# Value groups of the past behind score blocks, and two of the last eight output tiles on GpSimd

## The chip, the cores and the metric

The kernel runs on one core of one Trainium2 chip, in one launch. The metric is the device time of a whole execution in microseconds (us). Before the change three runs took 1004.15, 1002.61 and 1003.99 us, with a median of 1003.99 us. The profile comes from a further execution of 1003.43 us; its span, from the first to the last recorded instruction, is 1001.8 us, so 1.63 us lie around the span. The mean granted clock of TensorE was 0.998 of full speed.

TensorE (PE) multiplies; a matmul `out<-moving,weights` takes its weights as an array tile, written 128\*128 for the whole array, 64\*128 or 128\*32 for a part of it. VectorE (DVE), ScalarE (ACT) and GpSimd (POOL) work elementwise, SyncE (SP) issues DMAs, and ACT and POOL issue some too.

## The reference

The program computes one inference step of one decoder layer for 512 prompt tokens and 8 samples that share the weights:

```
m  = silu(c) @ ada_w + ada_b                  # shifts, scales, gates
h  = rms_norm(x) * (1 + scale1) + shift1
xr, gr, q, k, v, fl, ga, gb = split(h @ w_in)
ya = (rg_lru(conv(xr)) * gelu(gr)) @ w_proj_a                 # recurrence
yb = forgetting_attention(q, k, v, log_sigmoid(fl)) @ w_proj_b
x  = x + gate1 * ((sigmoid(ga) * ya + sigmoid(gb) * yb) @ w_o)
x  = x + gate2 * swiglu(rms_norm(x) * (1 + scale2) + shift2)
y  = rms_norm(x)
```

The prompt attends to itself, causally. Each of the 8 samples attends to 1024 past rows, which lie in 8 pages of 128 rows each, picked out of `cache_k` and `cache_v` by a page table, and to its own row:

```
s = q . k_all * scale + (decay of the forget gates)
p = softmax(s);   o = p @ v_all
```

The change touches `p @ v_all` for the past of the samples, and the last line, `y = rms_norm(x)`.

## The kernel before, in words

Prompt and samples stand side by side as 520 columns; the 1024 features are 8 tiles of 128 rows. A product of the layer (`product`, line 326) makes one tile of 128 output rows in two halves of 260 columns each. Its numbers are split into a rounded high part and a low rest, so each product is the sum of three: high by high, low by high and high by low. A half has 24 matmuls (`part_product`, L311): 8 steps of depth with three matmuls each.

The past of the samples runs beside these products. Its value pages come in pairs (one page for each of two samples, 512 KB each). A pair is used by one **value group**: `sample_values` (L946) issues 4 matmuls with 32 weight columns each, in array tiles 128\*32, for 512 moving columns (the profile counts 8). 32 groups are to be done, 8 for each of four pairs of samples; after a pair of samples `fold_values` folds the sum (one matmul, recorded as two, tile `pvs`).

What sets the order of the groups: the program is written out in order, and each engine runs its instructions in that order. Every product begins with `begin` (L289); for product n up to 41 it calls `tick(KEYS[n], n in VALUES)`. `tick` (L874) first moves the softmax of the past one step on (its small matmuls write tiles `lgt`, `lgm`, `lgs`), then issues one value group if one is due and its probabilities are there, and then up to KEYS[n] key pages, which DVE multiplies and sums (L857, L858). Right behind a value group the loads of the next pair are issued (`value_pages`, `page_load`): by POOL's queue up to n = 41, by SP's after that. Key pages, value pages and some weights share 7 buffers (`pgp`, tag `pg`), so a load waits until the buffer's last user is done.

From n = 42 on, in a loop over the 8 tiles of the attention, `at(i, part)` takes the place of `begin`'s call; the table VALUES_AT[i][part] says whether a group stands there. Round i of the loop runs on PE in this order:

1. first half of `k` of the next tile; four transposes `vt`; **part 0**; second half of `k`
2. eight transposes `ptt` of the probabilities (`turn(i, 0)`); **part 1**
3. first half of `v`; twelve more `ptt`; score block `sc` 0 and 1 of the next tile; **part 2**; second half of `v`
4. the weighted values `po` (`values`, L1412); score blocks `sc` 2 and 3 of the next tile; **part 3**

Scores and the recurrence's gate products (`gate`, L1130) use array tiles of 64\*128, the products and the transposes the whole 128\*128. After a score block DVE adds the decay and takes the minimum (L1362), ACT takes the exponential (L1363), DVE the reciprocal of the sums (L1365), and ACT, for one head of two POOL, scales the probabilities `p` (L1369), which the transposes `ptt` read.

The end of the kernel is `last_product` (L1671): the last product `fo`, its residual and the final norm, first for 280 columns and then for the 240 others. `norm(1)` gets the sums of squares by PE, their root by ACT (L1710), the reciprocal by DVE, and spreads the factor over 128 rows by PE into the PSUM tile `r3p` (L1715). Then DVE makes the eight tiles of `y` (L1726), two at a time, and SP issues a store for every two (L1727).

Of the kernel before, what the change touches and what calls it, by code (L numbers as in the profile page):

```python
# [12 lines left out]
ALU = mybir.AluOpType  # L13
# [54 lines left out]
def kernel(ctx, tc, xT, par1, par, gates, b_f, cst, cse, own, cache_k, cache_v, cache_lf, pt,  # L68
# [3 lines left out]
    pe, act, dve, pool, sp = nc.tensor, nc.scalar, nc.vector, nc.gpsimd, nc.sync  # L72
# [9 lines left out]
    def slot(name, cols=NT, dt=F32, parts=128):  # L82
        return heap.tile([parts, cols], dt, name=name, tag="slot")

    def bank(name, parts=128, cols=512):
        return psp.tile([parts, cols], F32, name=name, tag="bank")

    def small(name, parts, cols, bufs=4):
        return sm.tile([parts, cols], F32, name=name, tag="s_" + name, bufs=bufs)
# [6 lines left out]
    x = []  # L96
# [97 lines left out]
    def flush():  # L194
        while stores:
            sp.dma_start(*stores.pop(0))
# [2 lines left out]

    KEYS = dict(zip(range(42), (2, 2, 0, 0, 1, 2, 2, 2, 1, 1, 1, 1, 2, 2, 2, 1, 0, 1, 0, 1, 2, 2, 2, 2, 1, 1, 1, 1, 2, 2, 1, 2,  # L200
                                1, 1, 1, 2, 1, 1, 1, 1, 2, 0)))
    VALUES = (19, 21, 23, 25, 27, 29, 31, 35, 37, 39)
    LAST_POOL = 41

    def load_chunks(upto):
        while state["dma"] < len(chunks) and state["dma"] <= upto:
            c = state["dma"]
            if c in joined:
                raw = pgp.tile([128, GROUP, 256], F32, name="wraw", tag="pg")
            else:  # L210
                raw = wp.tile([128, KT, 256], F32, name="wraw", tag="wraw", bufs=2)
            o = 0
            for src, r0, nk, c0, n in chunks[c]:
                sp.dma_start(raw[:, :nk, o:o + n],
                             src[r0:r0 + nk * 128, c0:c0 + n].rearrange("(k p) c -> p k c", p=128))
                o += n
            raws[c] = raw
            state["dma"] += 1
# [59 lines left out]
    def reach(n, last, time):  # L278
        while n < last:
            time -= 1.34 if isinstance(units[n + 1][1], str) else 0.67 * units[n + 1][2]  # L280
            if time < 0:
                break
            n += 1
        return n
# [4 lines left out]
    def begin(last=None):  # L289
        n = state["n"]  # L290
        state["n"] += 1
        last = len(units) - 1 if last is None else last
        if n == 1:
            split_upto(reach(n, last, state["lead"]))
        if n < 42:
            tick(KEYS[n], n in VALUES)
        load_chunks(units[reach(n, last, state["load"])][0])
        split_upto(reach(n, last, state["lead"]))
        flush()
        return n  # L300
# [4 lines left out]
    def part_product(n, t0, t1, a, out, mid=None):  # L305
        hi, lo = splits[n]
        nk = units[n][2]
        for k in range(nk):
            ah, al = a(k) if callable(a) else (v[:, t0:t1] for v in a[k])
            for m, (wt, at) in enumerate(((hi, ah), (lo, ah), (hi, al))):  # L310
                state["mm"] = pe.matmul(out[:, :t1 - t0], lhsT=wt[k], rhs=at, start=k == 0 and m == 0,  # L311
                                        stop=k == nk - 1 and m == 2)
            if mid is not None and k == nk // 2 - 1:
                mid()
# [280 lines left out]
    for f in range(KT):  # L595
        t = slot("sq1")
# [50 lines left out]
    for n in range(6):  # L647
        t0, t1 = HALVES[n % 2]
# [19 lines left out]
    for n in range(6):  # L668
        t0, t1 = HALVES[n % 2]
# [204 lines left out]
    def tick(keys, values):  # L874
        state["age"] = 1 if state["n"] < 5 else 2
        key_sums()
        with in_place():
            for c in list(chains):
                c[0] += 1
                if c[0] >= 2:  # L880
                    c[0] = 0
                    if next(c[1], True):
                        chains.remove(c)
            state["due"] += values
            state["due"] -= some_values(min(1, state["due"]))
        value_pages()
        key_pages(keys)
# [141 lines left out]
    for i in range(KT):  # L1029
        if i % 4 == 0:  # L1030
            qtp.append(bank(f"qt{i}", NS))
        if i < 6:
            t = qpart[i]
# [15 lines left out]
        else:  # L1049
            t = slot("q")  # L1050
# [435 lines left out]
    scores(0, (2, 3))  # L1486
    g = None
    state.update(load=14, lead=8)
    VALUES_AT = [(1, 1, 0, 1)] * 4 + [(1, 1, 0, 0)] + [(1, 1, 0, 1)] * 2 + [(1, 1, 0, 0)]
    KEYS_AT = [(0, 0, 2, 0)] * 3 + [(0, 0, 0, 0)] * 5  # L1490

    def at(i, part):
        tick(KEYS_AT[i][part], VALUES_AT[i][part])
        flush()
# [176 lines left out]
    def last_product(ac):  # L1671
        ss3, r3 = slot("ss3"), slot("r3")
        squares = []
        u = state["n"]

        def done(i, j, t0, t1, b):
            gate, n = mod[:, 5, i], min(t1, NP) - t0
            if j == 0:
                t = small("rs", 128, NS)
                dve.tensor_tensor(t, b[:, n:t1 - t0], gate[:, 1:9], ALU.mult)  # L1680
            dve.scalar_tensor_tensor(x[i][:, t0:t0 + n], b[:, :n], gate[:, 0:1], x[i][:, t0:t0 + n],
                                     ALU.mult, ALU.add)
            if j == 0:
                dve.tensor_tensor(x[i][:, NP:], x[i][:, NP:], t, ALU.add)
            if i == 0:
                act.activation(ss3[:, t0:t1], x[i][:, t0:t1], AF.Square)
            else:
                q_ = heap.tile([128, t1 - t0], F32, name="sq3", tag="slot")
                act.activation(q_, x[i][:, t0:t1], AF.Square)
                if j == 0 or i < 6:  # L1690
                    (pool if j == 0 and i < 5 else dve).tensor_tensor(ss3[:, t0:t1], ss3[:, t0:t1], q_, ALU.add)
                else:
                    squares.append(q_)
            act.activation(x[i][:, t0:t1], x[i][:, t0:t1], AF.Copy, scale=prm[:, i, P_NF:P_NF + 1])

        def norm(j, t0, t1):
            n = t1 - t0
            parts = [ss3[:, t0:t1], *squares]
            r = bank("r3p")[:, :n] if j else r3[:, t0:t1]
            if j:  # L1700
                h_ = n // 2
                ps = [bank(f"r3_{b}", h_, 1) for b in range(2)]
                for k, q_ in enumerate(parts):
                    for b in range(2):
                        pe.matmul(ps[b], lhsT=q_[:, h_ * b:h_ * b + h_], rhs=ones[:, :1], start=k == 0,
                                  stop=k == len(parts) - 1)
                rt = small("rt", h_, 2, 1)
                dg = slot("dg", n, parts=h_)
                for b in range(2):
                    act.activation(rt[:, b:b + 1], ps[b], AF.Sqrt, bias=eps[:h_], scale=1.0 / D)  # L1710
                dve.reciprocal(rt, rt)
                for b in range(2):
                    bs = slice(h_ * b, h_ * b + h_)
                    dve.tensor_scalar(dg[:, bs], ident[:h_, :h_], rt[:, b:b + 1], None, ALU.mult)
                    pe.matmul(r[:, bs], lhsT=ones[:h_, :], rhs=dg[:, bs], start=True, stop=True)  # L1715
            else:
                ps = bank(f"r3_{j}")[:, :n]
                for k, q_ in enumerate(parts):
                    pe.matmul(ps, lhsT=ones, rhs=q_, start=k == 0, stop=k == len(parts) - 1)
                act.activation(r3[:, t0:t1], ps, AF.Sqrt, bias=eps, scale=1.0 / D)  # L1720
                dve.reciprocal(r, r3[:, t0:t1])
            eng = dve if j else pool
            for f0, f1 in ((0, 2), (2, 4), (4, 6), (6, 8)) if j else ((0, 2), (2, 5), (5, 8)):
                y = pgp.tile([128, 3, n], F32, name="y", tag="pg")
                for f in range(f0, f1):
                    eng.tensor_tensor(y[:, f - f0], x[f][:, t0:t1], r, ALU.mult)  # L1726
                sp.dma_start(yT[128 * f0:128 * f1, t0:t1].rearrange("(f p) t -> p f t", p=128), y[:, :f1 - f0])  # L1727

        for j, (t0, t1) in enumerate(LAST_PARTS):
            for i in range(KT):  # L1730
                if j == 0:
                    begin(u + KT - 1)
                b = bank(f"fo{i}_{j}")
                part_product(u + i, t0, t1, ac, b)
                done(i, j, t0, t1, b)
                if j and i == 0:
                    norm(0, *LAST_PARTS[0])
        norm(1, *LAST_PARTS[1])

    def pair_out():  # L1740
# [180 lines left out]
```

## Time and profile before

| what | us |
|---|---|
| runs (three) | 1004.15, 1002.61, 1003.99 |
| profiled execution | 1003.43 |
| its span | 1001.8 |
| PE busy | 984.8 (98% of the span) |
| DVE busy | 778.0 (78%) |
| ACT busy | 553.4 (55%) |
| POOL busy | 344.0 (34%) |

A row of the timeline gives the start of a run of equal instructions, its length, the engine, the line, the operation and its operands, how many there are (x4), and in brackets how long the engine stood idle before it and for whom. Matmuls are pipelined: the length of one is not what it costs. What one costs PE is the distance from its start to the start of the next. A group of instructions (by line or by tile) has the durations of one instruction in ns, least, median and most.

### The profile page before, as it was taken

Reading aid. Unit: us, or ns where it says so; the run is one execution under the profiler, and the core shown is the slowest. Engines: PE = TensorE matmul, PEld = TensorE weight load, DVE = VectorE, ACT = ScalarE, POOL = GpSimd, SP = SyncE. Lnnn points to the kernel's source line nnn. Section 1 sums busy time; section 2 is a strip of 40 time slices with the busy share of each in tenths; the row PEclk is TensorE's granted clock in tenths of the full one; section 3 lists DMA queues with packets and bytes.
Section 4 is the critical chain, followed back from the end, with each engine's and each line's share of the span. In section 5 each row is a group of like instructions: output and inputs, shape, how many; then the busy total and the mean of one; then the engine's idle time right before and its main releaser. Section 6 shows DMA issues by size and latency. Waiting matters only on the chain.

```text
span 1001.8 us, 21578 instructions
## 1 busy us (share of the span) xinstructions
PE 984.8 (98%) x8156; PEld 912.1 (91%) x8156; DVE 778.0 (78%) x1386; ACT 553.4 (55%) x1139; POOL 344.0 (34%) x436
## 2 busy tenths in 40 slices
PE   6999999999999999999999999999999999999996
PEld 5889999999898988888888879999999999999996
DVE  5598999979999878785564545868888888889864
ACT  5434769776951576767772224544444444445553
POOL 0254131323253266554310002394343342434212
PEclk9999999999999999999999999999999999999999
DMA  9998766879879999896667994242424234233212
GB/s 322 330 277 293 228 199 189 278 250 301 266 245 355 329 285 306 284 293 228 215 240 266 338 345 134 59 126 64 126 65 127 82 109 114 56 106 106 64 64 86
DMA packets 164507, 204.04 MB, mean 204 GB/s; under 512 B 9635, under 2 KB 128051, under 8 KB 164339
## 3 DMA queue, kind: packets, MB, share of 16 engines
q1 hardware_dynamic: 148162, 151.14, 48.2%
q0 software_dynamic: 12560, 45.10, 13.3%
q10 hardware_dynamic: 3680, 6.42, 1.7%
q8 instruction: 64, 1.05, 0.4%
q14 instruction: 41, 0.33, 0.1%
HBM read 189.54 MB, written 13.09 MB: 202 GB/s over the span
## 4 chain that ended last, share of the span: by engine, by line
PE 92%; ACT 4%; DVE 2%; DMA 1%; issue 1%; SPq 0%; DVEq 0%; ACTq 0%
PE fo L311 13%; PE wo L311 5%; PE gb L311 5%; PE pa L311 5%; PE xr L311 5%; PE pb L311 4%; PE v L311 4%; PE k L311 4%; PE ga L311 4%; PE gr L311 4%; PE pv L946 3%; PE po L1412 2%; PE sc L1349 2%; PE ada L378 2%; PE ptt L1378 2%; PE fi L311 1%
## 5 line engine op out<-in xcount | busy, mean ns | idle before, releaser
L250 ACT CAST whi<-wraw 128x1024 fp32r<-128x1024 f32 (+1 forms) x79 | 82.0, 1040 | 87.1 <-PE pb L311 34.4
L252 DVE TENSOR_TENSOR wlo<-wraw,whi 128x1024 fp32r<-128x1024 f32 (+1 forms) x79 | 97.4, 1233 | 20.3 <-ACT whi L250 16.9
L274 ACT CAST wb<-ws 128x512 fp32r<-128x512 f32 x72 | 44.7, 621 | 88.7 <-PE fo L311 61.8
L311 PE MATMUL fo<-ach,wb 128*128 128x260 f32 x512 | 93.4, 282 | 0.0
L275 DVE TENSOR_TENSOR wb<-wraw,wb 128x512 fp32r<-128x512 f32 x86 | 78.4, 912 | 5.5 <-ACT wb L274 4.9
L311 PEld LDWEIGHTS fo<-ach,wb 128*128 128x128 f32 x512 | 78.8, 188 | 0.0
L265 POOL TENSOR_TENSOR ws<-wraw 128x512 f32<-128x512 f32 x18 | 23.6, 1313 | 151.9 <-DMA wraw<-in_w_fi_dram 97.4
L794 POOL DMA_DIRECT2D pg<-in_cache_k_dram x70 | 37.8, 540 | 100.7 <-DVE S L858 55.5
L311 PE MATMUL fo<-acl,wb 128*128 128x260 f32 x256 | 72.2, 282 | 0.0
L274 ACT CAST wb<-wraw 128x512 fp32r<-128x512 f32 x86 | 53.5, 623 | 33.3 <-ACT cp L1808 6.4
L275 DVE TENSOR_TENSOR wb<-ws,wb 128x512 fp32r<-128x512 f32 x72 | 58.7, 815 | 12.5 <-ACT wb L274 11.0
L857 DVE TENSOR_TENSOR pg<-pg,qb 128x1024 f32<-128x1024 f32 x48 | 59.0, 1243 | 1.2 <-DMA pg<-in_cache_k_dram 1.2
L858 DVE TENSOR_REDUCE S<-pg 128x16 f32<-128x1024 f32 x48 | 57.4, 1209 | 0.2
L1369 POOL TENSOR_SCALAR p<-p,mu 128x128 f32<-128x128 f32 (+3 forms) x28 | 34.4, 1240 | 60.7 <-DVE mu L1365 49.7
L311 PEld LDWEIGHTS fo<-acl,wb 128*128 128x128 f32 x256 | 48.1, 188 | 0.0
L1363 ACT ACTIVATE p<-p,mu 128x128 f32<-128x128 f32 (+3 forms) x64 | 35.4, 554 | 18.3 <-DVE mu L1362 18.0
L311 PE MATMUL v<-hh,whi 128*128 128x260 f32 x128 | 37.7, 295 | 0.2
L311 PE MATMUL k<-hh,whi 128*128 128x260 f32 x128 | 37.6, 294 | 0.0
L311 PE MATMUL gb<-hh,whi 128*128 128x260 f32 x128 | 37.4, 292 | 0.0
L311 PE MATMUL pb<-oh,whi 128*128 128x260 f32 x128 | 37.0, 289 | 0.2 <-ACT oh L1470 0.2
L311 PE MATMUL ga<-hh,whi 128*128 128x260 f32 x128 | 36.6, 286 | 0.4 <-ACT tA L1192 0.4
L407 POOL TENSOR_TENSOR ss<-ss,sq 128x260 f32<-128x260 f32 x10 | 7.8, 781 | 84.9 <-ACT sq L406 84.6
(1122 smaller groups left out, 3958.8 us busy)
## 6 DMA issues: line engine op xcount, KB each, us to landing
wraw<-in_w_fi_dram SPq DMA_DIRECT2D x44, 512.0 KB, 4.5
pg<-in_cache_k_dram POOLq DMA_DIRECT2D x42, 512.0 KB, 5.7
pg<-in_cache_v_dram SPq DMA_DIRECT2D x42, 512.0 KB, 5.2
araw<-in_ada_w_dram SPq DMA_DIRECT2D x38, 512.0 KB, 6.9
wraw<-in_w_in_dram SPq DMA_DIRECT2D x28, 512.0 KB, 6.5
wraw<-in_w_in_dram SPq DMA_DIRECT2D x11, 1024.0 KB, 9.4
pg<-in_cache_v_dram POOLq DMA_DIRECT2D x22, 512.0 KB, 6.4
wraw<-in_w_fo_dram SPq DMA_DIRECT2D x16, 512.0 KB, 5.7
```

The costliest lines, as they stand in the source:

```text
L250: state["act"] = act.copy(hi[:, :k1 - k0], src)
L252: state["last"] = dve.tensor_tensor(lo[:, :k1 - k0], src, hi[:, :k1 - k0].bitcast(F32), ALU.subtract)
L265: pool.tensor_tensor(s1, a21, a22, ALU.add)
L274: state["act"] = act.copy(t[:, :4], src)
L275: state["last"] = dve.tensor_tensor(t[:, 4:], src, t[:, :4].bitcast(F32), ALU.subtract)
L311: state["mm"] = pe.matmul(out[:, :t1 - t0], lhsT=wt[k], rhs=at, start=k == 0 and m == 0, stop=k == nk - 1 and m == 2)
L794: done.append(eng.dma_start(pg, cache[bass.ds(r, 1), :, c0:c1].rearrange("a p c -> (a p) c")))
L857: dve.tensor_tensor(pg, pg, q, ALU.mult)
L858: last = dve.tensor_reduce(S[r // 2][:, c:c + H], pg.rearrange("p (h d) -> p h d", d=DH), AX.X, ALU.add)
L946: pe.matmul(pv[0][32 * gq:32 * gq + 32, :], lhsT=pw[r][:, c:c + 32], rhs=pgs[gq // 2][:, 512 * hf:512 * hf + 512], start=j == 0, stop=j == ...
L1363: act.activation(p[:, :n + 128], p[:, :n + 128], AF.Exp, bias=mu[:, 0:1], scale=-1.0, accum_out=mu[:, 1:2])
L1369: (pool.tensor_scalar(p, p, mu[:, 2:3], None, ALU.mult) if a and i + 1 < KT else act.activation(p, p, AF.Copy, scale=mu[:, 2:3]))
```

## The change

Three edits. The first moves two value groups among the products up to n = 41: the group of product 23 to product 22, and that of product 27 to product 28. The second rewrites VALUES_AT: in the rounds 0 to 3, 5 and 6 the group leaves part 0 and one stands at part 2; in round 4 the groups leave parts 0 and 1 and stand at parts 2 and 3; round 7 stays. The third is in `norm(1)`: ACT copies the factor `r3p` into SBUF, GpSimd makes tiles 6 and 7 of `y` from the copy, DVE makes the six others, and the store of tiles 6 and 7 is issued by ACT.

```diff
-    VALUES = (19, 21, 23, 25, 27, 29, 31, 35, 37, 39)
+    VALUES = (19, 21, 22, 25, 28, 29, 31, 35, 37, 39)
...
-    VALUES_AT = [(1, 1, 0, 1)] * 4 + [(1, 1, 0, 0)] + [(1, 1, 0, 1)] * 2 + [(1, 1, 0, 0)]
+    VALUES_AT = [(0, 1, 1, 1)] * 4 + [(0, 0, 1, 1)] + [(0, 1, 1, 1)] * 2 + [(1, 1, 0, 0)]
...
-            eng = dve if j else pool
-            for f0, f1 in ((0, 2), (2, 4), (4, 6), (6, 8)) if j else ((0, 2), (2, 5), (5, 8)):
+            if j:
+                copy = slot("r3", n)
+                act.copy(copy, r)
+            for f0, f1 in ((6, 8), (0, 2), (2, 4), (4, 6)) if j else ((0, 2), (2, 5), (5, 8)):
                 y = pgp.tile([128, 3, n], F32, name="y", tag="pg")
+                eng, fac = (dve, r) if j and f0 < 6 else (pool, copy if j else r)
                 for f in range(f0, f1):
-                    eng.tensor_tensor(y[:, f - f0], x[f][:, t0:t1], r, ALU.mult)
-                sp.dma_start(yT[128 * f0:128 * f1, t0:t1].rearrange("(f p) t -> p f t", p=128), y[:, :f1 - f0])
+                    eng.tensor_tensor(y[:, f - f0], x[f][:, t0:t1], fac, ALU.mult)
+                (act if j and f0 == 6 else sp).dma_start(yT[128 * f0:128 * f1, t0:t1].rearrange("(f p) t -> p f t", p=128), y[:, :f1 - f0])
```

On PE, in round 1 of the loop, before the change, at part 0 (`vt` are the four transposes of the values, `pv` is the value group, `k_1` the second half of `k`):

```order
2662 L311 MATMUL k_0_5816<-hl,whi 128x260
2663 L1303 MATMUL vt_5844<-cs,vt 128x128 x4
2664 L946 MATMUL pv_4881<-pg,pw 32x512 x4
2665 L311 MATMUL k_1_5881<-hh,whi 128x260
2666 L311 MATMUL k_1_5881<-hh,wlo 128x260
```

On PE at the same place after the change:

```order
2662 L311 MATMUL k_0_5816<-hl,whi 128x260
2663 L1303 MATMUL vt_5844<-cs,vt 128x128 x4
2664 L311 MATMUL k_1_5855<-hh,whi 128x260
2665 L311 MATMUL k_1_5855<-hh,wlo 128x260
2666 L311 MATMUL k_1_5855<-hl,whi 128x260
```

The group is gone from between the transposes and the product. On PE at part 2 of the same round before the change (`sc_1` is score block 1, one for each of two heads, `v_1` the second half of `v`):

```order
2740 L1349 MATMUL sc_1_6034<-kl,qq 128x256
2741 L1349 MATMUL sc_1_6035<-kl,qq 128x256
2742 L1349 MATMUL sc_1_6034<-kh,ql 128x256
2743 L1349 MATMUL sc_1_6035<-kh,ql 128x256
2744 L311 MATMUL v_1_6075<-hh,whi 128x260
```

On PE at part 2 after it:

```order
2740 L1349 MATMUL sc_1_6009<-kl,qq 128x256
2741 L1349 MATMUL sc_1_6008<-kh,ql 128x256
2742 L1349 MATMUL sc_1_6009<-kh,ql 128x256
2743 L946 MATMUL pv_4881<-pg,pw 32x512 x4
2744 L311 MATMUL v_1_6075<-hh,whi 128x260
```

The group now stands between the score block and the product. On PE at product 22 before the change (`gate` are the recurrence's gate products, `gb` a product):

```order
1456 L1130 MATMUL gate_0_1_3326<-xcl,gws 128x260
1457 L1130 MATMUL gate_1_1_3327<-xcl,gws 128x260
1458 L311 MATMUL gb_0_3375<-hh,whi 128x260
1459 L311 MATMUL gb_0_3375<-hh,wlo 128x260
1460 L311 MATMUL gb_0_3375<-hl,whi 128x260
```

On PE at product 22 after it:

```order
1456 L1130 MATMUL gate_0_1_3326<-xcl,gws 128x260
1457 L1130 MATMUL gate_1_1_3327<-xcl,gws 128x260
1458 L946 MATMUL pv_2982<-pg,pw 32x512 x4
1459 L311 MATMUL gb_0_3401<-hh,whi 128x260
1460 L311 MATMUL gb_0_3401<-hh,wlo 128x260
```

The group, which stood 48 product matmuls further down between two products, now follows the gate products.

## Rows read from the trace of the kernel before

**Rows 1.** The page's chain that ended last, by engine.

```profile
PE 92%; ACT 4%; DVE 2%; DMA 1%; issue 1%; SPq 0%; DVEq 0%; ACTq 0%
```

**Rows 2.** Busy time by engine, attention loop: busy (instructions) PE, PEld, DVE, ACT, POOL; clock, DMA.

```profile
344.00:518.00 174.00, 173.83 (x1426) 145.92 (x1425) 124.90 (x287) 126.56 (x312) 82.23 (x117) 1.00 0.82 265
```

**Rows 3.** Timeline of PE at product 23: a group between two products.

```profile
215.66 0.28 PE L311 MATMUL gb<-hh,wlo 128*128 128x260 f32 x1
215.78 0.28 PE L311 MATMUL gb<-hl,whi 128*128 128x260 f32 x1
215.99 1.06 PE L946 MATMUL pv<-pg,pw 128*32 128x512 f32 x8
216.98 0.39 PE L311 MATMUL gb<-hh,whi 128*128 128x260 f32 x1
217.21 0.28 PE L311 MATMUL gb<-hh,wlo 128*128 128x260 f32 x1
```

**Rows 4.** Timeline of PE, loop: score block before a product, and before a group.

```profile
342.71 0.39 PE L1349 MATMUL sc<-kh,ql 64*128 64x512 f32 x2
343.03 0.39 PE L311 MATMUL k<-hh,whi 128*128 128x260 f32 x1
343.25 0.28 PE L311 MATMUL k<-hh,wlo 128*128 128x260 f32 x1
...
364.99 0.40 PE L1349 MATMUL sc<-kh,ql 64*128 64x512 f32 x2
365.32 1.07 PE L946 MATMUL pv<-pg,pw 128*32 128x512 f32 x8
```

**Rows 5.** Timeline of PE: four transposes before a group (loop), and before a product (later).

```profile
369.31 0.60 PE L1303 MATMUL vt<-cs,vt 128*128 128x128 f32 x4
369.84 1.06 PE L946 MATMUL pv<-pg,pw 128*32 128x512 f32 x8
...
609.01 0.60 PE L390 MATMUL adat<-cs,adas 128*128 128x128 f32 x4
609.36 0.37 PE L311 MATMUL wo<-mixh,whs 128*128 128x260 f32 x1
609.56 0.28 PE L311 MATMUL wo<-mixh,whi 128*128 128x260 f32 x1
```

**Rows 6.** Timeline of PE: gate products before a group.

```profile
201.94 0.29 PE L1130 MATMUL gate<-xcl,gws 64*128 64x260 f32 x2
202.17 1.06 PE L946 MATMUL pv<-pg,pw 128*32 128x512 f32 x8
```

**Rows 7.** Timeline of PE: the first matmul of product 29, behind its value group.

```profile
258.17 0.39 PE L311 MATMUL ga<-hh,whi 128*128 128x260 f32 x1 [0.39 <-ACT tA L1192]
```

**Rows 8.** Timeline of PE and DVE at the end: root sums, factor and `y`.

```profile
994.43 0.70 PE L1715 MATMUL r3p<-dg,cs 120*128 120x120 f32 x4 [0.87 <-DVE dg L1714]
995.17 2.61 DVE L1726 TENSOR_TENSOR y<-x,r3p 128x240 f32<-128x240 f32 x8 [0.60 <-PE r3p L1715]
```

**Rows 9.** Timeline of SP's queue at the end: the stores of `y`.

```profile
995.92 2.26 SPq L1727 DMA_DIRECT2D out_yT_dram<-y  x4
```

**Rows 10.** Groups of instructions, by line or tile: ns least/median/most, first and last start.

```profile
L1726 POOL TENSOR_TENSOR y<-x,r x8: 781/784/990, 980.9 to 986.7; 128x280 f32<-128x280 f32 x8
L1273 ACT COPY kt<-k x16: 368/381/402, 286.6 to 488.0; 128x260 f32<-128x260 f32 x16
L1691 DVE TENSOR_TENSOR ss<-ss,sq x8: 408/450/812, 973.1 to 988.9; 128x240 f32<-128x240 f32 x5, 128x280 f32<-128x280 f32 x3
L1681 DVE SCALAR_TENSOR_TENSOR x<-fo,mod,x x16: 371/478/495, 959.5 to 992.0; 128x272 f32<-128x272 f32 x8, 128x240 f32<-128x240 f32 x8
```

**Rows 11.** Timeline of PE: a group whose pages came late.

```profile
307.91 1.93 PE L946 MATMUL pv<-pg,pw 128*32 128x512 f32 x8
```

**Rows 12.** Timeline of ACT and PE, round 4: the last scaled probabilities and their transposes.

```profile
439.91 1.23 ACT L1369 ACTIVATE p<-p,mu 128x384 f32<-128x384 f32 x2 [0.25 <-DVE mu L1365]
...
442.23 1.03 PE L1378 MATMUL ptt<-cs,p 128*128 128x128 f32 x8
```

## The prediction

> **What bounds the kernel now.** I read the page's chain first. It says which engine the end waited for: PE holds 92% of it [rows 1], so time is won where PE issues sooner, or in the last microseconds, where others hold the chain. Next come the engines' busy times in the attention loop, where eight of the ten moved groups stand: PE is busy for 173.83 of 174 us, DVE for 124.90, ACT for 126.56, POOL for 82.23 [rows 2]. Nobody is waited for there, so a saving on PE passes through one for one until another engine comes late. "Busy" hides what a change of work costs, though, because matmuls overlap. That is read from the timeline of PE, as the distance from one start to the next.
>
> **What a value group costs by its place.** Between two products, a group begins 0.21 us after the last product matmul (215.78 to 215.99), where two product matmuls are 0.12 apart (215.66 to 215.78). The next product begins 0.99 after the group's start, and its second matmul another 0.23 after its first instead of 0.12 [rows 3]. So beside its own 0.99 the group costs 0.09 on entry and 0.11 on exit, 0.20 in all.
>
> Behind a score block the same costs are already paid. From the last pair of score matmuls to a product it takes 0.32, and that product's second matmul comes after 0.22; from the same pair to a group it takes 0.33, and the product behind the group has the 0.23 of rows 3 [rows 4]. A group put there adds its own 0.99 and 0.02.
>
> Behind transposes the opposite holds. From the first of four transposes it takes 0.53 to a group, but 0.35 to a product, whose second matmul comes 0.20 later [rows 5]. The loop shows no transposes in front of a product at this place; the row is of the same form (four transposes 128x128, the whole array, then a product), later in the kernel. A group between transposes and product costs 0.18 on entry and 0.23 - 0.20 = 0.03 on exit, 0.21 in all.
>
> **Loop.** Eight groups leave transposes (seven behind `vt`, one behind `ptt`) and eight come in behind score blocks. Each saves 0.21 - 0.02 = 0.19; eight save 1.5 us, all of it on the path. Bounds: at most 8 x 0.21 = 1.7, if a score block takes a group for nothing; at least 0.2, if product matmuls behind the loop's transposes need the same 0.53 as a group does and only the 0.03 is left.
>
> What else a moved group carries: the loads of its next two pages (512 KB each), which SP issues in the loop and POOL before it. Both queues have 0% of the chain [rows 1], and the pages are wanted one group later, so I cost the issues at nothing; if that cover goes, the price is that of a late page, among the rivals. In round 0 the folding of a pair of samples goes along with its group, to behind `ptt`; it is the same two recorded matmuls between a group and a product, so nothing changes. No engine gets a new wait in the loop.
>
> **Products up to n = 42.** Two groups go from between products to behind gate products. These use array tiles 64\*128 like the scores, and the last pair of them stands 0.23 before a group [rows 6]; I take it that the group replaces the product's entry there as behind scores. Each saves 0.20, two 0.40. But PE is not the only one waited for here: at product 29, behind both places, PE stands idle for 0.39, until ACT has released tile `tA` [rows 7]. What PE gains ahead of that is lost in this wait unless ACT comes sooner too. Bounds 0 and 0.4; I take the middle, 0.2, since the product that the first move brings forward is itself evacuated by ACT.
>
> **The end.** The factor is there at 995.17, and DVE makes eight tiles in 2.61 us [rows 8], about 0.33 apart. SP issues four stores over 2.26 us from 995.92 [rows 9]; a DVE tile pair takes 0.63 to 0.66, so the third is issued about 0.63 before the fourth. With six tiles on DVE, SP's last store is the third, at 997.2 (the fourth begins when DVE's last tile ends, 995.17 + 2.61 = 997.8). ACT's copy of the factor, by the row of a slightly wider PSUM copy, takes 0.38; GpSimd's tile of 280 columns takes 784 ns, the first of a row 990 [rows 10], so by columns 0.85 and 0.67 for 240, together 1.52. With three hand-offs of about 0.03 (rows 8 and 9: the first two tiles end near 995.9, their store is issued at 995.92) ACT's store starts at 995.17 + 0.38 + 1.52 + 0.1 = 997.2. Both paths then end 0.6 before the old one. The order of the two does not matter.
>
> Bounds here: the cover is that DVE and GpSimd don't hinder each other. A DVE addition with two SBUF inputs took 408 ns at least and 812 at most in the stretch where GpSimd made its first eight tiles; the residual `x`, which like `y` takes one input from PSUM, stayed between 371 and 495 through the same stretch [rows 10]. `y` is of the second kind, so I take no hindrance. If DVE doubled all the same while GpSimd works (1.5 us), its third store would come 0.75 later, 0.1 after the old fourth. If GpSimd's tiles both took 990, 0.2 would be left of the gain. So 0.6, between -0.1 and 0.65.
>
> **Sum.** 1.5 + 0.2 + 0.6 = 2.3 us off. Against the profiled execution's own 1003.43 that is 1001.1; the median of the runs is 0.56 higher, which would give 1001.7. I take the middle, **1001.4**. What hides the moved loads: a pair of pages is loaded one group ahead, and with part 0 empty the groups stand further apart (in round 1 the one at 369.84 goes, and the next stands behind the second half of `k` and eight transposes), so transfers get more time, not less.
>
> **Rivals.**
>
> *The saving is that of one change of tile a move.* Before, each pair of places has three changes of the array's tile: into the group, out of it, and out of the score block. After, it has two, since the score block goes over into the group. If each move saves that one change at the price of rows 3 (0.09) and nothing else, the loop saves 8 x 0.09 = 0.7 and the early products up to 0.2, of which I take 0.1; with the end's 0.6 that is 1.4, so about 1002.3. Against it stand rows 5, where the step from transposes to a product is 0.18 shorter than that into a group, twice the 0.09. For it: those rows are from another stage. Chance 0.2.
>
> The Trainium skill has this as a rule (page "TensorEngine Tiling (Array Packing)", section "Tiling Modes"): a change of the tiling mode, not of the tile alone, drains the engine. By that rule the step from a score block to a group, a change too, is as dear as the one from a score block to a product; the trace agrees, with 0.33 and 0.32 [rows 4].
>
> *The end gives nothing*: the two engines hinder each other, or ACT's store lands late. 1.7 off remain, less 0.1: 1002.1. Rows 10 speak against it; that no DVE `y` ran beside a GpSimd `y` before leaves it open. Chance 0.12.
>
> *The shortened way from scores to transposes.* In each of these rounds the group that leaves part 0 also goes out of the time that the softmax has. In round 4 ACT ends the last scaling at 439.91 + 1.23 = 441.14, and PE wants the probabilities at 442.23 [rows 12]: 1.09 to spare, and the move takes 0.99 + 0.2 = 1.19 out of it. If the softmax does not start earlier, PE waits 0.1 there. For more, several rounds would have to lose half of their saving: 0.8 in all, 1002.2. Against it: the group at part 2 gives DVE 1 us more before the next score block, so that its queue is shorter. Chance 0.1.
>
> *Slower: late pages.* One group before the loop stood 1.93 instead of 1.06 on PE [rows 3, 11], so a late pair costs 0.87. Loads now wait at other places in SP's queue, behind score blocks, and what is queued behind a waiting load (weights, `q` tiles, decay rows) waits with it. Where three groups are late (2.6), the gain is gone; from six on (5.2) it is 1001.4 + 5.2 = 1006.6, slower by over 0.2%. Against it speaks the wider distance of the groups. Chance 0.08.
>
> **How the numbers follow.** The forecast has 0.5. A measurement of this kernel can tell about 0.2%, 2.0 us, from no change, so the border is 1002.0 against the median. Of the forecast's 0.5 about 0.42 lie below it; of the three rivals with less gain (0.42 together) about 0.1, since each is centred at the border or above; of the last none. That makes faster 0.53, and slower 0.06, most of the last rival; same has the other 0.41. The range's lower end takes the full bounds from below, 1.7 + 0.4 + 0.65 = 2.75 off 1003.43, and rounds down a little, 1000.4. The upper end is the median less 0.6, where two of the rivals meet, 1003.4. Late pages lie outside.
>
> **What would show it.** In the profile after: `vt` to `k` some 0.35 after the first transpose (right) or 0.53 (wrong); score pair to group 0.33, and the product's second matmul 0.23 after its first; PE's busy share in the loop unchanged and the loop 1.5 us shorter; at `ptt` of round 4 no idle time over 0.1. In front, the wait of 0.39 for `tA` grows to 0.6 or 0.8 if the early moves are lost. At the end, six `y` of DVE near 0.40 each, two of GpSimd under 0.9, and the last store issued near 997.2 less the time won before. The prediction is wrong if PE waits for page transfers, or if the end of the span stands as far behind `r3p` as before.

## The result and the profile after

The changed kernel takes 1005.63 us, median of 14 runs (1004.85 to 1007.23); the kernel before takes 1003.39, median of 14 (1002.61 to 1004.24). The ratio is 1.0023, with a 95% interval of 1.0015 to 1.0032: the medians lie 2.2 us apart, and the change is slower. The prediction was 1001.4, faster, with a range from 1000.4 to 1003.4. The profiled execution has a span of 1004.0 instead of 1001.8.

Where the time went is seen in two steps. PE reaches the last small products, `r3p`, at 992.31, where it stood at 994.43 before [rows 8]: up to there the kernel is 2.1 us faster. From there to the end of the span it takes 11.7 us instead of 7.4. The end loses 4.3. The 2.1 in front are what the two tables were to bring (1.7) and some luck: the late group at 307.9 [rows 11] took 1.49 here instead of 1.93, and that group stands where it stood. With it taken out, 1.7 are left.

```profile
307.80 1.49 PE L946 MATMUL pv<-pg,pw 128*32 128x512 f32 x8
```

PE's timeline at part 2 of round 1, the kernel before, and then at parts 0 and 2 of the same round after, answering to [rows 4, 5]:

```profile
380.84 0.28 PE L1349 MATMUL sc<-kh,ql 64*128 64x256 f32 x2
381.05 0.38 PE L311 MATMUL v<-hh,whi 128*128 128x260 f32 x1
381.27 0.28 PE L311 MATMUL v<-hh,wlo 128*128 128x260 f32 x1
```

```profile
368.26 0.60 PE L1303 MATMUL vt<-cs,vt 128*128 128x128 f32 x4
368.61 0.37 PE L311 MATMUL k<-hh,whi 128*128 128x260 f32 x1
368.81 0.28 PE L311 MATMUL k<-hh,wlo 128*128 128x260 f32 x1
...
378.62 0.28 PE L1349 MATMUL sc<-kh,ql 64*128 64x256 f32 x2
378.83 1.06 PE L946 MATMUL pv<-pg,pw 128*32 128x512 f32 x8
379.83 0.39 PE L311 MATMUL v<-hh,whi 128*128 128x260 f32 x1
380.06 0.28 PE L311 MATMUL v<-hh,wlo 128*128 128x260 f32 x1
```

From the first transpose to the product it now takes 0.35, with 0.20 to the second matmul; the pair of the shorter score block 1 goes over into the group in 0.21, as it went over into the product before, and the product follows 1.00 later, with 0.23 to its second matmul (0.22 before). The forecast had 0.35 and 0.20, and for the group behind scores nothing but its own 0.99 and 0.02.

The end, by the timelines of PE, ACT, DVE, GpSimd and the two issuing queues, answering to [rows 8, 9]:

```profile
992.31 0.70 PE L1715 MATMUL r3p<-dg,cs 120*128 120x120 f32 x4 [0.87 <-DVE dg L1714]
993.05 0.36 ACT L1724 COPY r<-r3p 128x240 f32<-128x240 f32 x1 [1.31 <-PE r3p L1715]
993.44 1.97 DVE L1729 TENSOR_TENSOR y<-x,r3p 128x240 f32<-128x240 f32 x6 [1.00 <-ACT r L1724]
993.49 1.34 POOL L1729 TENSOR_TENSOR y<-x,r 128x240 f32<-128x240 f32 x2 [8.18 <-ACT r L1724]
994.19 1.63 SPq L1730 DMA_DIRECT2D out_yT_dram<-y  x3
994.86 0.44 ACTq L1730 DMA_DIRECT2D out_yT_dram<-y  x1
```

All computing is over at 995.41 and all stores are issued by 995.82, against 997.78 and 998.18 before. Yet the span ends later. The chain of waits ends with this row and says nothing of what follows:

```profile
994.16 1.25 DVE y L1729 x4
```

8.6 us lie between its end and the end of the span (4.0 before: 995.17 + 2.61 = 997.78, span 1001.8). What fills them stands in no busy time and in no chain, since it is a queue's instruction. It is shown by the view of one source line, here `with tile.TileContext(nc) as tc:`, whose block is the whole kernel: the instructions that close the program carry this line. Columns as for other groups: least, median and most ns, first and last start. Of the kernel before:

```profile
L1905 POOLq DRAIN  x3: 46/104/14789, 981.0 to 1001.5; - x3
L1905 SPq DRAIN  x3: 7/7/7, 1000.9 to 1001.2; - x3
```

Of the kernel after:

```profile
L1908 POOLq DRAIN  x3: 46/104/9719, 993.5 to 1003.7; - x3
L1908 SPq DRAIN  x3: 7/7/7, 999.2 to 1003.4; - x3
```

GpSimd's queue closes with drains; the longest of the three is the one that waits for its work, and its row begins at about the start of the last tiles. Before, it ran from 981.0 for 14.79, to 995.8, which is 8.35 after the end of the last `y` tile on GpSimd (980.89 + 6.56 = 987.45). SP, with the stores landed, came to its own drain at 1000.9, so this was hidden by 5 us. After, it ran from 993.5 for 9.72, to 1003.2, again 8.35 after GpSimd's last tile. SP was ready at 999.2 and waited for 4 us.

### The profile page after: what moved, and what is told of

It reads as the page before. It is cut to its first block, busy times and chain, and to the rows that moved or that the text cites. A ratio compares the mean times of both kernels' runs of the same rounds, so it can differ in the third digit from the quotient of the medians.

```text
span 1004.0 us, 21571 instructions
## 1 busy us (share of the span) xinstructions
PE 981.6 (98%) x8156; PEld 911.8 (91%) x8156; DVE 776.0 (77%) x1384; ACT 554.2 (55%) x1140; POOL 346.0 (34%) x438
## 4 chain that ended last, share of the span: by engine, by line
PE 79%; DVE 7%; ACT 5%; issue 4%; DMA 2%; POOL 0%; POOLq 0%; SPq 0%; DVEq 0%; ACTq 0%
PE fo L311 13%; PE wo L311 5%; PE pa L311 5%; PE pb L311 4%; PE v L311 4%; PE k L311 4%; PE pv L946 3%; PE gb L311 2%; PE po L1412 2%; PE sc L1349 2%; PE ga L311 2%; PE ptt L1378 2%; PE ada L378 2%; DVE pg L857 2%; PE fi L311 1%
```

## The experiments

The theory after this reading: GpSimd's closing drain ends 8.35 us after its last tensor instruction, whatever that is, and counts where that is later than the stores' end. The rivals: the moved groups cost something hidden; the store from ACT's queue holds the end up; the drain grows with GpSimd's work. Each ratio below is to the kernel before, run beside it; the chip is not the same in all experiments.

**The tables alone** (of the kernel before, both tables changed and nothing else):

```diff
-    VALUES = (19, 21, 23, 25, 27, 29, 31, 35, 37, 39)
+    VALUES = (19, 21, 22, 25, 28, 29, 31, 35, 37, 39)
-    VALUES_AT = [(1, 1, 0, 1)] * 4 + [(1, 1, 0, 0)] + [(1, 1, 0, 1)] * 2 + [(1, 1, 0, 0)]
+    VALUES_AT = [(0, 1, 1, 1)] * 4 + [(0, 0, 1, 1)] + [(0, 1, 1, 1)] * 2 + [(1, 1, 0, 0)]
```

> Both tables of the change (VALUES, VALUES_AT), the end as before. Theory (the tables win what was forecast, and the loss is the closing drain of GpSimd's queue, which ends 8.35 us after its last tensor instruction): with GpSimd's last work back near 985 the drain is over near 994 and hidden; PE stands 2.1 us earlier at the root's sums, the span is about 999.7, the time 1001.3, some 2.1 below before. Rival (the moved groups cost something that the distance of the products does not show): the time stays at or above before, 1003.4 or more.

Measured: 1001.31, ratio 0.9980 (0.9971 to 0.9989). The tables win 1.9 us, and the loss is not theirs.

**The end alone** (the changed kernel with both tables of before):

```diff
-    VALUES = (19, 21, 22, 25, 28, 29, 31, 35, 37, 39)
+    VALUES = (19, 21, 23, 25, 27, 29, 31, 35, 37, 39)
-    VALUES_AT = [(0, 1, 1, 1)] * 4 + [(0, 0, 1, 1)] + [(0, 1, 1, 1)] * 2 + [(1, 1, 0, 0)]
+    VALUES_AT = [(1, 1, 0, 1)] * 4 + [(1, 1, 0, 0)] + [(1, 1, 0, 1)] * 2 + [(1, 1, 0, 0)]
```

> The new end alone, both tables as before. Theory (drain): GpSimd's two tiles end near 997.0, the drain 8.35 later at 1005.3, the span 0.8 behind that, 1006.1, the time 1007.7, some 4.3 above before. Rival (the new end is worth 0.6 as forecast, and the loss comes from the tables): 1002.8.

Measured: 1007.28, ratio 1.0038 (1.0024 to 1.0051), 4.1 us slower. GpSimd's last tiles in its timeline, and the drains of its closing line:

```profile
995.34 1.34 POOL L1729 TENSOR_TENSOR y<-x,r 128x240 f32<-128x240 f32 x2 [8.15 <-ACT r L1724]
```

```profile
L1908 POOLq DRAIN  x3: 46/104/9717, 995.3 to 1005.6; - x3
L1908 SPq DRAIN  x3: 7/7/7, 1001.1 to 1005.3; - x3
```

996.68 + 8.35 = 1005.03, and the drain ends at 995.3 + 9.72 = 1005.0.

**ACT's store without GpSimd** (the tables alone, and in `norm(1)`):

```diff
-            for f0, f1 in ((0, 2), (2, 4), (4, 6), (6, 8)) if j else ((0, 2), (2, 5), (5, 8)):
+            for f0, f1 in ((6, 8), (0, 2), (2, 4), (4, 6)) if j else ((0, 2), (2, 5), (5, 8)):
-                sp.dma_start(yT[128 * f0:128 * f1, t0:t1]...
+                (act if j and f0 == 6 else sp).dma_start(yT[128 * f0:128 * f1, t0:t1]...
```

> Both tables of the change; tiles 6 and 7 stand first and their store goes from ACT's queue, but DVE makes them from the PSUM factor like all others: no copy, nothing on GpSimd. Theory (drain of GpSimd): like the tables alone, 1001.3. Rival (the store from ACT's queue holds the end up, by its landing or its queue's closing): 1004 to 1005.6.

Measured: 1001.46, ratio 0.9980 (0.9971 to 0.9989), like the tables alone. ACT's queue is cleared of it.

**A tiny GpSimd instruction, late** (the tables alone, and in `norm(1)`, behind the diagonal):

```diff
+            if j:
+                pool.tensor_copy(small("tiny", h_, 8, 1), dg[:, n - 8:])
```

> Both tables, the end as before, and beside it one GpSimd copy of 120x8 numbers, which nobody reads, once DVE has made the diagonal of the roots (near 992.4). Theory (the drain ends 8.35 us after GpSimd's last tensor instruction, whatever its size): the copy ends near 992.7, the drain near 1001.0, the span at 1001.9, the time 1003.5, about 2 above the tables alone. Rival (the drain grows with the work, or needs the contention with DVE): no cost, 1001.3.

Measured: 1003.21, ratio 1.0000 (0.9991 to 1.0009): the gain of the tables is gone, by an instruction of 0.19 us that nothing waits for. Its row in the timeline, and the drains:

```profile
992.20 0.19 POOL L1723 COPY tiny<-dg 120x8 f32<-120x8 f32 x1 [7.20 <-DVE dg L1714]
```

```profile
L1907 POOLq DRAIN  x3: 46/104/8559, 992.2 to 1001.3; - x3
L1907 SPq DRAIN  x3: 7/7/7, 999.0 to 1001.0; - x3
```

992.39 + 8.35 = 1000.74; the drain ends at 992.2 + 8.56. The size of the work plays no part here: 8.35 behind this copy as behind the tiles.

**The same instruction, 2 us earlier** (as before, but it copies from a tile that is ready sooner):

```diff
+            if j:
+                pool.tensor_copy(small("tiny", 128, 8, 1), x[KT - 2][:, t0:t0 + 8])
```

> Both tables, the end as before, and the copy of 8 columns by GpSimd once more, but of the residual's tile 6, which is ready near 989.3 instead of 992.3. Theory (the drain ends 8.35 us after the last tensor instruction and counts only where that is later than the stores' end, near 998.7): it ends near 989.5, the drain near 997.9, hidden: 1001.3, like the tables alone. Rival (any GpSimd instruction this late costs): 1003.2, like the later copy.

Measured: 1001.81, ratio 0.9985 (0.9976 to 0.9994). The interval holds the ratio of the tables alone, and not the late copy's 1.0000, though it touches the late copy's interval. The rows show it better:

```profile
990.07 0.19 POOL L1723 COPY tiny<-x 128x8 f32<-128x8 f32 x1 [4.07 <-ACT x L1694]
```

```profile
L1907 POOLq DRAIN  x3: 46/104/8557, 990.0 to 1000.1; - x3
L1907 SPq DRAIN  x3: 7/7/7, 999.5 to 999.8; - x3
```

The drain ends at 998.6, before SP's at 999.5: hidden, with 0.9 to spare. So GpSimd's last instruction costs nothing as long as it ends at least 8.35 us before SP comes to its drain. Over all these runs:

| kernel | GpSimd's last work ends | its drain ends | SP's drain | span |
|---|---|---|---|---|
| before | 987.46 | 995.80 | 1000.98 | 1001.8 |
| after | 994.82 | 1003.17 | 999.26 | 1004.0 |
| end alone | 996.68 | 1005.02 | 1001.1 | 1005.8 |
| tiny, late | 992.40 | 1000.74 | 999.05 | 1001.6 |
| tiny, early | 990.26 | 998.61 | 999.55 | 1000.3 |
| tables alone | 984.88 | 993.22 | 998.65 | 999.5 |

Drain less work is 8.35 in each row (to 0.01), and the span is the later of the two drains plus 0.8. Why it is 8.35, no run here shows.

**The loop's table alone** (of the kernel before, only VALUES_AT changed, as in the first experiment):

> VALUES_AT alone changed; the groups of products 23 and 27 stay, the end as before. Theory (the loop gives the whole gain; the two early moves are lost again in PE's wait for tA): PE stands about 1.5 earlier behind the loop, the wait for tA stays at 0.4 instead of 0.6 to 0.7, and the time is that of both tables, 1001.3, or at most 0.2 above. Rival (each early move is worth its 0.2): 1001.7.

Measured: 1001.27, ratio 0.9984 (0.9975 to 0.9993). PE's first matmul of product 29 in this kernel:

```profile
258.28 0.39 PE L311 MATMUL ga<-hh,whi 128*128 128x260 f32 x1 [0.38 <-ACT tA L1192]
```

And with both tables:

```profile
258.18 0.39 PE L311 MATMUL ga<-hh,whi 128*128 128x260 f32 x1 [0.60 <-ACT tA L1192]
```

The wait for `tA` grows by 0.22 of the 0.4 that the early moves save (in the profile of the changed kernel by 0.33). The medians can't tell the rest, up to 0.2, from nothing.

**Stores of other sizes** (the tables alone, and in `norm(1)`):

```diff
-            for f0, f1 in ((0, 2), (2, 4), (4, 6), (6, 8)) if j else ((0, 2), (2, 5), (5, 8)):
+            for f0, f1 in ((0, 1), (1, 3), (3, 5), (5, 7), (7, 8)) if j else ((0, 2), (2, 5), (5, 8)):
-                sp.dma_start(yT[128 * f0:128 * f1, t0:t1]...
+                (act if j and f0 in (1, 5) else sp).dma_start(yT[128 * f0:128 * f1, t0:t1]...
```

> Both tables; DVE makes all eight last tiles of y, stored in groups of 1, 2, 2, 2 and 1 tiles, of which two from ACT's queue. With the drain hidden, the end hangs on the stores alone: the first is issued 0.3 earlier, the last carries one tile instead of two (0.1 to 0.3 less from issue to landing). If the stores' landing sets the end: 1000.9. If the number of stores at the end costs as much as it wins: 1001.3.

Measured: 1001.93, ratio 0.9987 (0.9978 to 0.9996): no gain that the runs show. From the first `y` to SP's drain it takes 5.7 against 5.8 with the tables alone, so 0.1 is what the sizes win in the trace.

**A wait that the tables bring.** In the changed kernel DVE and PE show, at the start of round 6, what was not there before:

```profile
477.33 0.15 DVE L1434 TENSOR_TENSOR mp<-mb,lf 16x8 f32<-16x8 f32 x1 [2.22 <-DMA mb<-mtd]
477.41 0.68 DVE L1416 TENSOR_TENSOR ol<-po,oh 64x512 fp32r<-64x512 f32 x1
```

```profile
478.15 0.39 PE L311 MATMUL k<-hh,whi 128*128 128x260 f32 x1 [0.41 <-DVE ol L1416]
```

The order of DVE had put one small addition, `mp`, ten recorded instructions further up, ahead of `ol`; there it waits 2.2 us for a DMA (`mb`, the past's maxima), `ol` behind it frees `po`'s bank later, and PE waits. In the eight profiles with VALUES_AT changed and `mp` at this place PE's wait was between 0.1 and 1.2 us. The experiment holds the addition back until the sum it is combined with is there (the tables alone, and in `join_weights`):

```diff
-        dve.tensor_scalar(sx, sn, DH ** -0.5, None, ALU.mult)
-        dve.tensor_tensor(mp, mb[:, 0], lf[:, NP:], ALU.add)
+        own_s = dve.tensor_scalar(sx, sn, DH ** -0.5, None, ALU.mult)
+        with tc.issue_after(own_s.ins):
+            dve.tensor_tensor(mp, mb[:, 0], lf[:, NP:], ALU.add)
```

> Both tables, the end as before, and one small DVE addition (mp, 16x8, which reads the past's maxima) held until the sum that it is combined with is there, near 500 instead of 477. With the moved groups DVE stood idle for 1.9 to 3.0 us before this addition, waiting for the DMA that brings the maxima, and PE behind it for 0 to 1.2 us (before the loop's k product, for DVE's rest of the values). Theory (that wait is a new one that the tables bring, by the place of the DMA in SP's queue): DVE's idle time there and PE's wait are gone; 0.3 to 0.5 below the tables alone, 1000.9. Rival (PE then waits for another engine at the same place): as the tables alone, 1001.3.

> The same kernel as e1_orders_only, on the same chip as the one with the late addition, for their comparison: 1001.3; PE's wait for the rest of the values between 0 and 0.7.

Measured: 1000.93 with the late addition, ratio 0.9980 (0.9971 to 0.9989); the tables alone again 1001.28, ratio 0.9985 (0.9976 to 0.9994), with a PE wait of 0.33 there. Busy times in the loop with the late addition:

```profile
344.00:518.00 174.00, 174.00 (x1440) 147.53 (x1439) 125.33 (x288) 127.44 (x311) 82.29 (x117) 1.00 0.85 269
```

And with the tables alone, on the same chip:

```profile
344.00:518.00 174.00, 173.67 (x1436) 147.11 (x1435) 126.10 (x288) 127.01 (x311) 82.02 (x117) 1.00 0.84 268
```

The wait is gone, 0.33 us of PE's time; the medians differ by as much, but the intervals of the ratios overlap, so the times don't show this gain.

## Why the prediction was wrong

*The loop: right, with two terms missed that nearly cancel.* 1.5 was forecast; from the first `vt` to the products behind the loop PE won 1.5 in the changed kernel (0.57 ahead, then 2.08), 1.3 with the loop's table alone, and 2.1 with the late addition. The prediction said "No engine gets a new wait in the loop"; the missed loss is the wait for `ol`. PE stands idle for 0.41 in the first of these, 0.74 in the second, not at all in the third. From the score pair in front of it to the product it takes 2.12, 2.46 and 1.56 (1.56 before), so the wait costs 0.56, 0.90 and nothing. The missed gain is at the two places where a small matmul of the past's softmax, `lgs`, stands behind the score block. PE of the kernel before, in round 5:

```profile
471.33 0.28 PE L1349 MATMUL sc<-kh,ql 64*128 64x256 f32 x2
471.54 0.22 PE L924 MATMUL lgs<-cs,mk 128*32 128x2 f32 x2
471.85 0.39 PE L311 MATMUL v<-hh,whi 128*128 128x260 f32 x1
```

And at the same place with the late addition:

```profile
467.67 0.28 PE L1349 MATMUL sc<-kh,ql 64*128 64x256 f32 x2
467.88 0.19 PE L924 MATMUL lgs<-cs,mk 128*32 128x2 f32 x1
467.89 0.63 PE L946 MATMUL pv<-pg,pw 128*32 128x512 f32 x3
467.93 0.17 PE L924 MATMUL lgs<-cs,mk 128*32 128x2 f32 x1
467.96 1.02 PE L946 MATMUL pv<-pg,pw 128*32 128x512 f32 x5
468.91 0.39 PE L311 MATMUL v<-hh,whi 128*128 128x260 f32 x1
```

From score pair to product it takes 1.24 instead of 0.52: the group adds 0.72 there and not 0.99, since `lgs`, of the same tile 128\*32, runs among its matmuls. 8 x 0.19 and 2 x 0.27 make 2.06, the measured 2.1; less the 0.56 of the wait that is the 1.5 of the changed kernel. In all nine profiles with the new VALUES_AT the gain and the cost of the wait add up to 2.1 or 2.2. The rival of one change of tile a move would have been 0.7, and is out.

*The early products: right within its bounds.* The forecast was 0.2 between 0 and 0.4. From the group at 202 to the wait for `tA` PE took 0.40 less (55.21 instead of 55.61), as the two moves were to save; with the tables alone the wait, 0.60 instead of 0.39, took back half of it, and in the profile of the changed kernel, with 0.72, most.

*The end: wrong, and this step decided.* The forecast was "Both paths then end 0.6 before the old one", with bounds of -0.1 and 0.65; it was 4.3 later. Of this 3.9 is GpSimd's drain and 0.4 a wait for a copy. Three things failed in that step. First, the sum stopped at the stores: it did not ask what else the program waits for before it ends. The closing drain of GpSimd's queue is 3.9 of the loss (1003.17 against SP's 999.26). It was there to be read in the trace of before, in the view of line L1905: the two rows above; the chain of waits and the busy times, which I read, don't hold it. Moving work to an idle engine moved that engine's last instruction from 5 us inside the cover to 4 us outside.

Second, DVE's six tiles began 0.39 after the factor was there, behind ACT's copy of the same PSUM tile: the program gave DVE's first `y` a wait for ACT in place of the one for PE. The sum had counted the copy on GpSimd's path alone. From `r3p`'s start to the first `y` it took 1.13 in the two kernels with the copy, and 0.74 before and with ACT's store without GpSimd. What the sum took for GpSimd's own tiles did no harm: 1.52, of which 0.85 for a slow first tile. The 990 ns of [rows 10] belonged to the second tile of its row, the first took 782, and the two tiles together took 1.34.

Third, issuing the last store sooner would not have helped by much. From the first issue to the last landing it took 4.56 to 4.57 before (995.92 to 1000.48), after (994.19 to 998.75) and with the tables alone (993.60 to 998.16). After the change the last store was issued 1.25 behind the first instead of 1.89, and landed 3.31 after its issue instead of 2.67. So the stores wait for each other's transfers. In the middle of the stretch the DMA engines are full, before and after (last two numbers: busy share of the DMA engines, GB/s); at this rate the 960 KB alone take about 2.8, an estimate:

```profile
998.00:999.00 1.00, 0.00 (x0) 0.00 (x0) 0.00 (x0) 0.00 (x0) 0.00 (x0) 0.50 1.07 353
```

```profile
996.00:997.00 1.00, 0.00 (x0) 0.00 (x0) 0.00 (x0) 0.00 (x0) 0.00 (x0) 0.50 1.05 357
```

So without the drain the new end would have been 0.4 longer than the old (SP's drain 6.95 after `r3p`'s start, 6.55 before), not 0.6 shorter.

*The rivals.* The one for the slower side named late pages; it did not come. The group at 307.9, whose page was late before [rows 11], was late again in most of the kernels, by up to 1.0, with its place unchanged, and 1.29 long in the end alone, where both tables are those of before. The shortened way of the softmax did not come either: in round 4 PE took up the probabilities at 439.47, 0.8 after ACT had them. DVE's and GpSimd's hindrance did not show: DVE's tiles took 396 ns at the median beside GpSimd, as alone, and GpSimd's two together 1.34. The new wait for `ol` was in no rival, though the order of DVE's instructions had the moved addition in it.

## What to carry to other kernels

Before work is given to an idle engine near the end, look up what closes the program on that engine's queue, and how long after its last instruction; the chain of waits doesn't show it when it is hidden. Where two engines make the last output, the sum has to end with the last transfer and the last queue, not with the last instruction. A table that moves work on one engine also reorders small instructions on others, so each engine's order is to be searched for something new ahead of what is waited for.

## What the runs showed of the hardware

GpSimd's queue needed 8.35 us to drain after its last tensor instruction, in every kernel, behind eight tiles of 280 columns as behind 8 columns. DVE's and ACT's drains ended with their work: in the kernel before at 997.8 and 993.9, where their last instructions end at 997.78 and 993.86.

The clock fell at the end, at a point that differs between kernels. The last small products run just there: with the tables alone they took 0.97 instead of 0.70, at a granted clock of 0.53 in this stretch (half is the lower of the two levels, 1.2 GHz):

```profile
992.00:994.00 2.00, 0.81 (x4) 0.53 (x4) 1.15 (x4) 0.00 (x0) 0.00 (x0) 0.53 0.00 0
```

With ACT's store and no GpSimd the clock was still whole in that stage:

```profile
990.00:992.00 2.00, 1.13 (x8) 0.97 (x8) 0.64 (x3) 0.84 (x3) 0.00 (x0) 1.00 0.00 0
```

In the 2 us before the first row PE had been busy for 0.87. The kernel of the tables alone, profiled twice, took 0.97 here once and 1.21 the other time. So some profiles hold 0.3 to 0.5 us here, and others none, without a cause in their code.
